# Two decoder layers on one core: V of two heads at once, a moved rope key, and another order of the sparse-attention items

## The chip, the cores and the metric

The kernel runs on one core of a Trainium2 chip. Times are device microseconds (us) of one launch. The names of the engines are those of the profile: PE is TensorE (PEld its weight load), DVE is VectorE, ACT is ScalarE, POOL is GpSimd, SP is the engine that issues most DMAs.

## What is computed

Two decoder layers over 512 tokens of width 1024, float32. Layer 0 mixes tokens with multi-head latent attention (MLA), layer 1 with sparse attention (an indexer picks 128 keys for each query). Each layer then attends to 256 memory tokens and runs a SwiGLU FFN; each sub-layer is followed by a scaled residual and a layer norm. Cut to the parts that the change touches:

```python
def mla_mixer(x, pos, w_in, q_norm, w_uq, kv_norm, w_ukv, w_o):
    h = x @ w_in
    c_q = h[..., :512]; c_kv = h[..., 512:768]; k_rope = h[..., 768:]
    q = rms_norm(c_q, q_norm) @ w_uq
    kv = rms_norm(c_kv, kv_norm) @ w_ukv
    ...

def dsa_mixer(x, pos, rel_bias, w_in, w_o):     # 16 heads, 4 KV heads
    ...
    _, sel = lax.top_k(score, 128)
    logits = einsum(q, k[sel]) * 64 ** -0.5 + rel_bias[bucket]
    o = softmax(logits) @ v[sel]
    return o @ w_o

def memory_cross_attention(x, mem, w_q, w_kv, w_o):   # 4 heads of 256
    q = (x @ w_q).reshape(b, s, 4, 256)
    kv = (mem @ w_kv).reshape(b, 256, 2, 4, 256)
    p = softmax(einsum(q, kv[:, :, 0]) * 256 ** -0.5)
    return einsum(p, kv[:, :, 1]).reshape(b, s, 1024) @ w_o
```

## The kernel before

Every large product is made of two fp32r parts: `split` (L98) lets ScalarE cast the high half (L99) and VectorE, or GpSimd where it is asked for, subtract the low half (L101), and `mm3` (L121) issues three matmuls, high by high (L122), high by low (L123) and low by high (L124). `chunk` (L108) loads a 128x1024 piece of a weight by a DMA on SP's queue into one of three `raw` buffers and splits it into `wh` and `wl` (five each). Working tiles come from the pools `t2` (39 of 128x512) and `t8` (9 of 128x2048); PSUM has four banks "a" and four banks "b". Each engine runs its instructions in the order in which the program was scheduled, and waits for its operands.

The front (from L169): x and the weight `w_ckv` come in slices, four steps `c` of two k-slices each; `ps2` are the four token tiles of c_kv and of the rope key (304 columns). `trig` (L449) makes sine and cosine on VectorE in steps. Then 8 copies on ScalarE (L521) and four transposes (L522) make the rope key `pkb`; four chunks of `w_cq` are loaded; for each token tile, 24 matmuls make `psq[tt]`, and `rms_t` (L527) normalises (L533) and transposes (L536) c_kv of this tile and c_q of the one before.

Cross-attention (`cross`, L733): for each head, `scores` with the softmax, the next head's Q projection (`q_proj`), the next head's K and V (`xa_kv`, L714), then `pv`, which first normalises and transposes P and then multiplies. K is two chunks of `xa_k`, V two chunks of `xa_v`; the V matmuls have 256 columns:

```python
        pv = bank("a", (P, 2, 256))
        for mt in range(2):
            for k in range(NK):
                mm3(pv[:, mt], ..., (w[0][:, k % 4], w[1][:, k % 4]), ...)
```

Sparse attention: 16 items of four heads each, item i is query tile i // 4 and KV head i % 4. `dsa_scores` (s) adds mask and bias and runs the softmax's first steps (L420 on VectorE, L426 on ScalarE), `dsa_t` (t) normalises, transposes (L1041) and splits P, `dsa_pv` (p) multiplies by V and sorts the heads (L1060 to L1077). The first items run inside the eight turns `j` that project Q: `steps` says which. In each turn five top-k steps of the masks (L978, L979) are put on VectorE, and `stack_q_pool` (L922) lets GpSimd subtract the low halves of two Q tiles (L927, L928):

```python
    steps = {2: "s0", 3: "t0", 4: "s1 p0", 5: "t1", 6: "s2 p1", 7: "t2"}
```

After the turns come s3, p2, s4, t3, and then the loop over the rest. `dsa_bias` (L1004) reads an item's bias from DRAM, for the first four items ahead of time into a `t2` tile, for the others at the scores into a `t8` tile.

## Time and profile before

| what | value |
|---|---|
| median of 3 runs | 1540.42 us (1538.08 to 1541.06) |
| the profiled execution | 1538.13 us |
| its span | 1536.3 us, 20733 instructions |
| PE busy | 1503.6 us (98%), 7902 matmul records |
| DVE busy | 994.9 us (65%) |
| ACT busy | 650.2 us (42%) |
| POOL busy | 303.9 us (20%) |
| DMA | 166.45 MB, mean 108 GB/s |

The page of a profile gives for each engine the time in which it was busy, and for groups of instructions their count, busy time and mean. A timeline row is one instruction or a run of equal ones: its start, its length, and in brackets how long the engine stood idle before and what released it. Matmuls are pipelined, so a matmul's own length is more than the step from one start to the next, and it is the steps that add up. PEclk is the clock that TensorE was granted, as a share of full speed.

### The profile page before, as it was taken

The numbers are of one execution on the slowest core, as the hardware profiler recorded it, in microseconds if no ns is written. First come the engines' busy times: TensorE is split into PE (matmuls) and PEld (weight loads), VectorE is DVE, ScalarE is ACT, GpSimd is POOL, SyncE is SP. The second block draws the span as 40 slices with busy tenths as digits, with TensorE's granted clock in tenths as the row PEclk, the third lists the DMA queues.
The fourth block names the chain that finished last, engine by engine and source line by source line (L and its number), as shares of the span: only waits on it lengthen the run. The fifth ranks groups of instructions, "written<-read, shape, count | busy, mean of one in ns | idle before, by whom it ended". The sixth has DMA issues, their size and how long they took to land.

```text
span 1536.3 us, 20733 instructions
## 1 busy us (share of the span) xinstructions
PE 1503.6 (98%) x7902; PEld 1283.5 (84%) x7902; DVE 994.9 (65%) x1741; ACT 650.2 (42%) x1158; POOL 303.9 (20%) x299
## 2 busy tenths in 40 slices
PE   8999999999999999999999989999999999999997
PEld 7788889988898888888888787898988888888886
DVE  7787868454746665654668988675448465656545
ACT  5677753343233333332246577344332433333230
POOL 1222001000032331400024653000002322324002
PEclk9999999999999999999999999999999999999999
DMA  6233424323333232233242147333323233222221
GB/s 214 71 98 107 155 83 134 125 85 97 124 97 101 77 124 97 96 97 108 84 138 87 51 158 240 110 119 102 110 94 125 83 110 98 102 94 90 97 96 55
DMA packets 51417, 166.45 MB, mean 108 GB/s; under 512 B 5300, under 2 KB 11972, under 8 KB 49268
## 3 DMA queue, kind: packets, MB, share of 16 engines
q1 hardware_dynamic: 50740, 164.18, 32.6%
q8 instruction: 62, 1.02, 0.3%
q10 hardware_dynamic: 576, 0.93, 0.2%
q14 instruction: 39, 0.32, 0.1%
HBM read 160.86 MB, written 9.47 MB: 111 GB/s over the span
## 4 chain that ended last, share of the span: by engine, by line
PE 88%; DVE 5%; ACT 3%; DMA 2%; issue 1%; POOL 1%; SPq 0%; POOLq 0%; DVEq 0%; ACTq 0%
PE ps L122 27%; PE ps L123 27%; PE ps L124 27%; DVE t L101 2%; PE ps L336 1%; ACT wh L99 1%; ACT t L426 1%; ACT t L99 1%; DMA raw<-in_w_cq_dram 1%; PE ps L1043 1%; PE ps L644 1%; DMA t<-in_xT_dram 1%; PE ps L1060 0%; POOL wl L101 0%; DMA t<-scr 0%
## 5 line engine op out<-in xcount | busy, mean ns | idle before, releaser
L122 PE MATMUL ps<-t,wh 128*128 128x512 f32 (+1 forms) x1256 | 456.2, 364 | 3.5 <-DVE t L101 3.4
L123 PE MATMUL ps<-t,wh 128*128 128x512 f32 (+1 forms) x1256 | 455.2, 362 | 0.8 <-DVE t L101 0.8
L124 PE MATMUL ps<-t,wl 128*128 128x512 f32 (+1 forms) x1256 | 454.9, 362 | 0.0
L99 ACT CAST wh<-raw 128x1024 fp32r<-128x1024 f32 (+3 forms) x219 | 227.4, 1038 | 450.0 <-PE ps L123 167.1
L101 DVE TENSOR_TENSOR wl<-raw,wh 128x1024 fp32r<-128x1024 f32 (+2 forms) x198 | 253.2, 1280 | 218.0 <-ACT wh L99 216.3
L122 PE MATMUL ps<-wh,t 128*128 128x512 f32 (+3 forms) x838 | 305.4, 364 | 1.1 <-ACT t L426 0.9
L123 PE MATMUL ps<-wl,t 128*128 128x512 f32 (+3 forms) x838 | 303.1, 362 | 1.2 <-DVE wl L101 1.2
L124 PE MATMUL ps<-wh,t 128*128 128x512 f32 (+3 forms) x838 | 303.0, 362 | 0.2 <-DVE t L101 0.2
L122 PEld LDWEIGHTS ps<-t,wh 128*128 128x128 f32 x1256 | 237.1, 189 | 41.5 <-DVE t L101 5.5
L123 PEld LDWEIGHTS ps<-t,wh 128*128 128x128 f32 x1256 | 237.2, 189 | 37.0 <-DVE t L101 1.3
L124 PEld LDWEIGHTS ps<-t,wl 128*128 128x128 f32 x1256 | 237.1, 189 | 36.6
L122 PEld LDWEIGHTS ps<-wh,t 128*128 128x128 f32 x838 | 158.5, 189 | 25.1 <-ACT t L426 1.3
L123 PEld LDWEIGHTS ps<-wl,t 128*128 128x128 f32 x838 | 158.4, 189 | 24.6 <-DVE wl L101 1.4
L124 PEld LDWEIGHTS ps<-wh,t 128*128 128x128 f32 x838 | 158.4, 189 | 24.0 <-DVE t L101 0.4
L99 ACT CAST t<-ps 128x512 fp32r<-128x512 f32 (+2 forms) x249 | 122.9, 525 | 129.3 <-PE ps L336 86.1
L279 POOL TENSOR_TENSOR sm<-sm,mhalf 128x1 f32<-128x1 f32 x32 | 28.6, 893 | 689.0 <-DVE sm L277 689.0
L101 DVE TENSOR_TENSOR t<-ps,t 128x512 fp32r<-128x512 f32 (+2 forms) x249 | 144.1, 607 | 20.3 <-ACT t L99 19.5
L99 ACT CAST wh<-t 128x1024 fp32r<-128x1024 f32 x56 | 58.9, 1052 | 141.9 <-PE ps L123 123.6
L101 DVE TENSOR_TENSOR wl<-t,wh 128x1024 fp32r<-128x1024 f32 x56 | 71.2, 1272 | 65.2 <-ACT wh L99 63.4
L863 DVE TENSOR_TENSOR t<-ps,t 128x512 f32<-128x512 f32 x44 | 30.4, 692 | 120.1 <-PE ps L124 120.1
L101 DVE TENSOR_TENSOR t<-t,t 128x512 fp32r<-128x512 f32 (+2 forms) x113 | 84.5, 751 | 23.0 <-ACT t L99 20.7
L99 ACT CAST t<-t 128x512 fp32r<-128x512 f32 (+2 forms) x113 | 64.5, 574 | 56.2 <-POOL t L797 33.6
(178 smaller groups left out, 1654.5 us busy)
## 6 DMA issues: line engine op xcount, KB each, us to landing
raw<-in_ffn_in_dram SPq DMA_DIRECT2D x88, 512.0 KB, 3.5
t<-in_ffn_dg_dram SPq DMA_DIRECT2D x16, 1024.0 KB, 5.0
raw<-in_xa_k_dram SPq DMA_DIRECT2D x16, 512.0 KB, 3.5
raw<-in_xa_v_dram SPq DMA_DIRECT2D x16, 512.0 KB, 3.9
raw<-in_xa_q_dram SPq DMA_DIRECT2D x16, 512.0 KB, 3.9
raw<-in_xa_o_dram SPq DMA_DIRECT2D x16, 512.0 KB, 3.4
raw<-in_ffn_dl_dram SPq DMA_DIRECT2D x12, 512.0 KB, 3.4
scr<-vscr SPq DMA_DIRECT2D x16, 319.5 KB, 4.4
```

What stands on the lines that cost most here:

```text
L99: nc.scalar.copy(h, src)
L101: (eng or nc.vector).tensor_tensor(l, src, h.bitcast(F32), op=ALU.subtract)
L122: nc.tensor.matmul(ps, st[0], mv[0], start=start, stop=False, skip_group_check=more)
L123: nc.tensor.matmul(ps, st[0], mv[1], start=False, stop=False, skip_group_check=more)
L124: nc.tensor.matmul(ps, st[1], mv[0], start=False, stop=stop, skip_group_check=more)
L279: nc.gpsimd.tensor_tensor(b, a, mhalf, op=ALU.pow)
L336: nc.tensor.transpose(pt[:, k], x_of(tt)[:, 512 * n + P * k:512 * n + P * k + P], ident)
L426: nc.scalar.activation(Sx, src, AF.Exp, bias=nb, scale=scale, accum_out=self.sm[:, i:i + 1])
L644: nc.tensor.transpose(pt[:, P * qt:P * qt + P], Ss[qt][:, P * kb:P * kb + P], ident)
L863: nc.vector.tensor_tensor(sg, pu, sg, op=ALU.mult)
L1043: nc.tensor.transpose(pt[:, P * i:P * i + P], Ss[i][:, P * kb:P * kb + P], ident)
```

## The change

Three parts. In the front, `w_ckv` is laid out with its eight k-slices side by side and loaded in four DMAs of 1, 2, 3 and 2 slices, all on ScalarE's queue, into the three `raw` buffers; the positions and constants are loaded right after x; and the rope key's copies and transposes become `rope_key()`, called after the first token tile's `psq` and `rms_t`. In cross-attention, `xa_kv` makes V for two heads at once (for an even head, four chunks of two k-slices by 512 columns), and `turned`, the normalise and transpose of P, runs before the next head's `xa_kv`, with only the products left in `pv`. In sparse attention, item 0 starts one turn later, item 4's bias is read at turn 4 into two `t2` tiles, and after the turns the order is s4, s3, s5, p2, t3, then the loop without its s5.

```diff
--- before.py
+++ after.py
@@ -167,20 +167,24 @@
...
-    def pairs_of(tile_):
-        return tile_[:, 0:2 * NC0].rearrange("p (k m) -> p k m", k=2)
-
-    raw_w = [pairs_of(wp.tile([P, 1024], F32, tag="raw", name=nm("raw"), bufs=3)) for _ in range(3)]
+    def threes(tag, dt, bufs=5):
+        ts = [wp.tile([P, 1024], dt, tag=tag, name=nm(tag), bufs=bufs) for _ in range(3)]
+        return [t[:, 0:3 * NC0].rearrange("p (k m) -> p k m", k=3) for t in ts]
+
+    raw_w = threes("raw", F32, 3)
     xr = A["xT"].rearrange("c p (k t) -> c p k t", k=2)
-    wr = A["w_ckv"].rearrange("c p (k m) -> c p k m", k=2)
-    for i in range(2):
+    wr = A["w_ckv"].rearrange("p (k m) -> p k m", k=NK)
+    for i, ks in enumerate((slice(0, 1), slice(1, 3))):
         nc.sync.dma_start(raw_x[0][:, i], xr[0, :, i])
-        nc.scalar.dma_start(raw_w[0][:, i], wr[0, :, i])
+        nc.scalar.dma_start(raw_w[0][:, ks], wr[:, ks])
     nc.sync.dma_start(raw_x[0][:, 2:4], xr[1])
-    nc.scalar.dma_start(raw_w[1], wr[1])
-    nc.scalar.dma_start(raw_w[2], wr[2])
+    nc.scalar.dma_start(raw_w[1], wr[:, 3:6])
     nc.sync.dma_start(raw_x[1][:, 0:2], xr[2])
+    nc.scalar.dma_start(raw_w[2][:, 0:2], wr[:, 6:8])
     nc.sync.dma_start(raw_x[1][:, 2:4], xr[3])
+    posi = t2(I32)
+    nc.sync.dma_start(posi, A["positions"].broadcast_to((P, S)))
+    nc.sync.dma_start(cst, A["consts"])
...
@@ -484,45 +488,44 @@
...
     ps2 = [bank("b") for _ in range(NT)]
+    whs, wls = threes("wh", FR), threes("wl", FR)
+    w_parts = {0: (0, 0, 1), 1: (0, 1, 3), 2: (1, 0, 3), 6: (2, 0, 2)}
     for c in range(4):
         h, l = XT[c // 2]
-        if c == 3:
-            raw_w.append(pairs_of(wp.tile([P, 1024], F32, tag="raw", name=nm("raw"), bufs=3)))
-            nc.sync.dma_start(raw_w[3], wr[3])
-        rx, rw = raw_x[c // 2], raw_w[c]
-        wh = pairs_of(wp.tile([P, 1024], FR, tag="wh", name=nm("wh")))
-        wl = pairs_of(wp.tile([P, 1024], FR, tag="wl", name=nm("wl")))
+        rx = raw_x[c // 2]
         step = 1 if c == 0 else 2
         for i in range(0, 2, step):
             k0 = 2 * (c % 2) + i
             split(h[:, k0:k0 + step], l[:, k0:k0 + step], rx[:, k0:k0 + step])
-            sw = slice(i, i + step)
-            split(wh[:, sw], wl[:, sw], rw[:, sw])
+            if 2 * c + i in w_parts:
+                t, a, b = w_parts[2 * c + i]
+                split(whs[t][:, a:b], wls[t][:, a:b], raw_w[t][:, a:b])
         for i in range(2):
             k = 2 * c + i
             xh, xl = k_of(XT, k)
             for tt in range(NT):
                 ts_ = ts_of(tt)
-                mm3(ps2[tt][:, 0:NC0], (xh[:, ts_], xl[:, ts_]), (wh[:, i], wl[:, i]), k == 0, k == NK - 1)
-    posi = t2(I32)
-    nc.sync.dma_start(posi, A["positions"].broadcast_to((P, S)))
-    nc.sync.dma_start(cst, A["consts"])
+                mm3(ps2[tt][:, 0:NC0], (xh[:, ts_], xl[:, ts_]), (whs[k // 3][:, k % 3], wls[k // 3][:, k % 3]),
+                    k == 0, k == NK - 1)
     steps = trig()
     for _ in range(2):
         next(steps)
...
-    pkb = bank("a")
-    for tt in range(NT):
-        kr = t2(F32, (P, 2, 2, 32))
-        for a in range(2):
-            c0 = 256 + 16 * a
-            nc.scalar.copy(kr[:, a], ps2[tt][:, c0:c0 + 32].unsqueeze(1).broadcast_to((P, 2, 32)))
-        nc.tensor.transpose(pkb[:, ts_of(tt)], kr.rearrange("p a b c -> p (a b c)"), ident)
     pk = t2()
-    nc.scalar.copy(pk, pkb)
     wcq = [chunk(A["w_cq"][c], (P, 2, 512)) for c in range(4)]
+
+    def rope_key():
+
+        pkb = bank("a")
+        for tt in range(NT):
+            kr = t2(F32, (P, 2, 2, 32))
+            for a in range(2):
+                c0 = 256 + 16 * a
+                nc.scalar.copy(kr[:, a], ps2[tt][:, c0:c0 + 32].unsqueeze(1).broadcast_to((P, 2, 32)))
+            nc.tensor.transpose(pkb[:, ts_of(tt)], kr.rearrange("p a b c -> p (a b c)"), ident)
+        nc.scalar.copy(pk, pkb)
...
@@ -569,6 +572,8 @@
         rms_t(ps2[tt], 256, tt, gkv[:, 0:256], ckv)
         if tt:
             rms_t(psq[tt - 1], 512, tt - 1, gq, cq)
+        if tt == 0:
+            rope_key()
         if tt < 2:
             next(steps)
@@ -719,15 +724,20 @@
...
-        ws = [chunk(A["xa_v"][i, hd, c], (P, 4, 256)) for c in range(2)]
-        pv = bank("a", (P, 2, 256))
-        for mt in range(2):
-            for k in range(NK):
+        if hd % 2:
+            return Kt, None
+        ws = [chunk(A["xa_v"][i, hd // 2, c], (P, 2, 512)) for c in range(4)]
+        pvs = [bank("a") for _ in range(2)]
+        for k in range(NK):
+            w = ws[k // 2]
+            for mt in range(2):
                 ms = slice(P * mt, P * mt + P)
-                w = ws[k // 4]
-                mm3(pv[:, mt], (m[k][0][:, ms], m[k][1][:, ms]), (w[0][:, k % 4], w[1][:, k % 4]), k == 0, k == NK - 1)
-        Vt = (t2(FR, (P, 2, 256)), t2(FR, (P, 2, 256)))
-        split(Vt[0], Vt[1], pv)
+                mm3(pvs[mt], (m[k][0][:, ms], m[k][1][:, ms]), (w[0][:, k % 2], w[1][:, k % 2]), k == 0, k == NK - 1)
+        Vt = []
+        for pv in pvs:
+            v = (t2(FR), t2(FR))
+            split(v[0], v[1], pv)
+            Vt.append(v)
         return Kt, Vt
@@ -756,9 +766,8 @@
...
-        def pv(hd, sx):
+        def turned(sx):
             Ss = sx.normalise()
-            Vt = kvs[hd][1]
             PT = []
...
+            return PT
+
+        def pv(hd, PT):
+            Vt = kvs[hd // 2 * 2][1]
             for dt in range(2):
                 po = bank("a")
-                ds_ = slice(P * dt, P * dt + P)
+                ds_ = slice(256 * (hd % 2) + P * dt, 256 * (hd % 2) + P * dt + P)
                 for mb in range(2):
-                    mm3(po, (Vt[0][:, mb, ds_], Vt[1][:, mb, ds_]), PT[mb], mb == 0, mb == 1)
+                    mm3(po, (Vt[mb][0][:, ds_], Vt[mb][1][:, ds_]), PT[mb], mb == 0, mb == 1)
...
@@ -781,8 +794,10 @@
             Ss = scores(hd, Q)
             if hd < 3:
                 Q = q_proj(hd + 1)
+            PT = turned(Ss)
+            if hd < 3:
                 kvs[hd + 1] = xa_kv(i, hd + 1, m)
-            pv(hd, Ss)
+            pv(hd, PT)
@@ -1004,11 +1019,17 @@
     def dsa_bias(qt, g):
         n = P * (qt + 1)
         c0 = 127 + 384 - 128 * qt
-        bt = t8(F32, (P, 4, 512)) if qt else t2(F32, (P, 4, P))
-        read = nc.sync.dma_start(bt[:, :, 0:n],
-                                 scr[bass.ds(r * (1 + qt), 1), 4 * g:4 * g + 4, :, c0:c0 + n].rearrange("a h p k -> p (a h) k"))
+        if (qt, g) == (1, 0):
+            bts = [t2(F32, (P, 2, 256)) for _ in range(2)]
+        else:
+            bts = [t8(F32, (P, 4, 512)) if qt else t2(F32, (P, 4, P))]
+        m = 4 // len(bts)
+        for i, bt in enumerate(bts):
+            read = nc.sync.dma_start(bt[:, :, 0:n],
+                                     scr[bass.ds(r * (1 + qt), 1), 4 * g + m * i:4 * g + m * i + m, :,
+                                         c0:c0 + n].rearrange("a h p k -> p (a h) k"))
         reads.append(read)
-        return bt
+        return [bts[i // m][:, i % m, 0:n] for i in range(4)]
@@ -1018,15 +1039,15 @@
         n = P * (qt + 1)
         N = max(n, 256)
         ts_ = slice(P * qt, P * qt + P)
-        bt = dsa_bias(qt, g) if qt else first_bias[g]
-        sx = Softmax([bt[:, i, 0:n] for i in range(4)])
+        bt = dsa_bias(qt, g) if 4 * qt + g > 4 else first_bias[4 * qt + g]
+        sx = Softmax(bt)
         for i in range(4):
             ps = bank("b")
...
-            sx.exp(i, ps[:, :n], 0.125, bt[:, i, 0:n])
+            sx.exp(i, ps[:, :n], 0.125, bt[i])
@@ -1091,7 +1112,7 @@
...
-    steps = {2: "s0", 3: "t0", 4: "s1 p0", 5: "t1", 6: "s2 p1", 7: "t2"}
+    steps = {3: "s0", 4: "t0 s1", 5: "p0 t1", 6: "s2 p1", 7: "t2"}
...
-        if j < 4:
-            first_bias.append(dsa_bias(0, j))
+        if j < 5:
+            first_bias.append(dsa_bias(j // 4, j % 4))
...
+    run_s(4)
     run_s(3)
+    run_s(5)
     run("p2")
-    run_s(4)
     run_t(3)
     for i in range(3, 16):
         a = 1 if i < LA else 0
         if i != LA:
-            run_s(i + 1 + a)
+            if i > 3:
+                run_s(i + 1 + a)
             run_t(i + a)
@@ -1170,7 +1193,8 @@
     w = I["mla_w_in"][0]
     f["w_cq"] = _tm(w[:, :512], 2, 512)[0]
-    f["w_ckv"] = _tm(np.concatenate([w[:, 512:800], w[:, 768:784]], 1), 2, NC0)[0]
+    ckr = np.concatenate([w[:, 512:800], w[:, 768:784]], 1)
+    f["w_ckv"] = ckr.reshape(NK, P, NC0).transpose(1, 0, 2).reshape(P, NK * NC0)
@@ -1194,7 +1218,7 @@
-    f["xa_v"] = np.stack([_tm(I["xa_w_kv"][i][:, 1024:], 4, 256) for i in range(2)])
+    f["xa_v"] = np.stack([_tm(I["xa_w_kv"][i][:, 1024:], 2, 512) for i in range(2)])
```

Line numbers of the changed kernel are some 3 to 21 higher from the rope key on (L420 is L424 there, L533 is L536, L1027 is L1048, L1041 is L1062, L1060 is L1081).

TensorE at the end of the c_kv products (`ps_130`, `ps_133`); before, the rope key's transposes (L522) stand between them and the first Q products (128x512):

```order
L124 MATMUL ps_130<-wh_227,t_10_118 128x304
L522 MATMUL ps_279<-ident,t_37_280 128x128
L522 MATMUL ps_279<-ident,t_38_284 128x128
L522 MATMUL ps_279<-ident,t_39_288 128x128
L122 MATMUL ps_322<-wh_300,t_7_115 128x512
L522 MATMUL ps_279<-ident,t_40_292 128x128
L123 MATMUL ps_322<-wl_301,t_7_115 128x512
```

and with the change:

```order
L124 MATMUL ps_133<-wh_136,t_11_121 128x304
L122 MATMUL ps_298<-wh_276,t_8_118 128x512
L123 MATMUL ps_298<-wl_277,t_8_118 128x512
L124 MATMUL ps_298<-wh_276,t_9_119 128x512
L122 MATMUL ps_298<-wh_276,t_8_118 128x512
L123 MATMUL ps_298<-wl_277,t_8_118 128x512
```

The four transposes have left this place; they now follow the first tile's 24 products and its two c_kv transposes.

VectorE at the same time; before, up to the low half of the fourth chunk of w_cq (`wl_319`; `wl_307` and `wl_313` are the second and third, lines 466 to 472 are steps of `trig`):

```order
L472 SCALAR_TENSOR_TENSOR t_32_261<-t_33_262,t_32_261 128x512
L101 TENSOR_TENSOR wl_307<-raw_304,wh_306 128x1024
L472 SCALAR_TENSOR_TENSOR t_32_261<-t_33_262,t_32_261 128x512 x2
L466 TENSOR_SCALAR t_33_262<-t_32_261 128x512
L101 TENSOR_TENSOR wl_313<-raw_310,wh_312 128x1024
L470 TENSOR_SCALAR t_33_262<-t_33_262 128x512
L472 SCALAR_TENSOR_TENSOR t_32_261<-t_33_262,t_32_261 128x512 x3
L101 TENSOR_TENSOR wl_319<-raw_316,wh_318 128x1024
```

and with the change (`wl_295` is the fourth chunk, `wl_283` and `wl_289` the second and third, the steps of `trig` have lines 470 to 476):

```order
L476 SCALAR_TENSOR_TENSOR t_29_255<-t_30_256,t_29_255 128x512
L101 TENSOR_TENSOR wl_289<-raw_286,wh_288 128x1024
L476 SCALAR_TENSOR_TENSOR t_29_255<-t_30_256,t_29_255 128x512 x2
L470 TENSOR_SCALAR t_30_256<-t_29_255 128x512
L474 TENSOR_SCALAR t_30_256<-t_30_256 128x512
L476 SCALAR_TENSOR_TENSOR t_29_255<-t_30_256,t_29_255 128x512 x2
L101 TENSOR_TENSOR wl_295<-raw_292,wh_294 128x1024
```

One of the last three steps of L472 (L476 now) has moved behind the fourth chunk; the other steps still stand ahead of it.

TensorE where the eight turns of sparse attention end; before, item 2's transposes (L1041), then item 3's scores (128x256, two matmuls for a head: L1027, L1028), with item 2's products (L1060) behind them:

```order
L1041 MATMUL ps_11567<-ident,t_1578_11099 128x128 x4
L1027 MATMUL ps_11579<-t_1554_10981,t_1667_11459 128x256
L1028 MATMUL ps_11579<-t_1554_10981,t_1667_11459 128x256
L1027 MATMUL ps_11584<-t_1554_10981,t_1668_11460 128x256
L1028 MATMUL ps_11584<-t_1554_10981,t_1668_11460 128x256
L1027 MATMUL ps_11589<-t_1554_10981,t_1693_11555 128x256
L1028 MATMUL ps_11589<-t_1554_10981,t_1693_11555 128x256
L105 MATMUL ps_11567<-t_1699_11572,identn 128x512
L1027 MATMUL ps_11594<-t_1554_10981,t_1694_11556 128x256
L1028 MATMUL ps_11594<-t_1554_10981,t_1694_11556 128x256
L1060 MATMUL ps_11603<-t_1699_11572,t_1454_10444 128x512
```

and with the change, where item 4's scores (three matmuls for a head: L1047 is the mask) come first:

```order
L1062 MATMUL ps_11469<-ident,t_1575_10997 128x128 x4
L1047 MATMUL ps_11481<-t_1537_10795,identr 128x256
L1048 MATMUL ps_11481<-t_1544_10833,t_1552_10888 128x256
L1049 MATMUL ps_11481<-t_1544_10833,t_1552_10888 128x256
L1047 MATMUL ps_11487<-t_1537_10795,identr 128x256
L1048 MATMUL ps_11487<-t_1544_10833,t_1552_10888 128x256
L1049 MATMUL ps_11487<-t_1544_10833,t_1552_10888 128x256
L1047 MATMUL ps_11493<-t_1537_10795,identr 128x256
L1048 MATMUL ps_11493<-t_1544_10833,t_1552_10888 128x256
L1049 MATMUL ps_11493<-t_1544_10833,t_1552_10888 128x256
L1047 MATMUL ps_11499<-t_1537_10795,identr 128x256
L1048 MATMUL ps_11499<-t_1544_10833,t_1552_10888 128x256
```

Item 3's scores follow behind these twelve matmuls.

## Rows read from the trace of the kernel before

**Rows 1.** The page: engines' busy time; two groups (count | busy us, mean ns)

```profile
PE 1503.6 (98%) x7902; PEld 1283.5 (84%) x7902; DVE 994.9 (65%) x1741; ACT 650.2 (42%) x1158; POOL 303.9 (20%) x299
...
L99 ACT CAST wh<-raw 128x1024 fp32r<-128x1024 f32 (+3 forms) x219 | 227.4, 1038 | 450.0 <-PE ps L123 167.1
...
L101 DVE TENSOR_TENSOR wl<-raw,wh 128x1024 fp32r<-128x1024 f32 (+2 forms) x198 | 253.2, 1280 | 218.0 <-ACT wh L99 216.3
```

**Rows 2.** Waits of TensorE: total us, times, longest us

```profile
PE ps L522 <- ACT t L521: 3.6, 1, 3.6
...
PE ps L1027 <- POOL t L927: 3.2, 2, 2.8
...
PE ps L123 <- DVE wl L101: 1.2, 1, 1.2
```

**Rows 3.** TensorE's timeline, front: start us, us, line, tiles [idle before <- releaser]

```profile
25.10 0.79 PE L522 MATMUL ps<-ident,t 128*128 128x128 f32 x3 [3.63 <-ACT t L521]
...
25.64 0.48 PE L122 MATMUL ps<-wh,t 128*128 128x512 f32 x1
...
29.46 0.42 PE L122 MATMUL ps<-wh,t 128*128 128x512 f32 x1
...
39.46 0.48 PE L122 MATMUL ps<-wh,t 128*128 128x512 f32 x1
```

**Rows 4.** Timelines of TensorE (one row) and GpSimd (two), sparse attention

```profile
889.53 0.49 PE L1027 MATMUL ps<-t,t 128*128 128x256 f32 x1 [2.77 <-POOL t L927]
...
888.22 1.26 POOL L927 TENSOR_TENSOR t<-t,t 64x512 fp32r<-64x512 f32 x1
...
889.55 1.27 POOL L928 TENSOR_TENSOR t<-t,t 64x512 fp32r<-64x512 f32 x1
```

**Rows 5.** Windows, front: us, busy us by engine, PEclk, DMA share, GB/s

```profile
2.00:12.00 10.00, 8.47 (x45) 7.46 (x46) 5.12 (x9) 6.79 (x10) 1.05 (x4) 1.00 0.97 356
12.00:38.00 26.00, 22.32 (x120) 19.31 (x119) 22.52 (x39) 13.01 (x29) 2.52 (x4) 0.93 0.54 178
26.00:30.00 4.00, 4.00 (x13) 3.13 (x12) 3.86 (x7) 1.90 (x6) 0.00 (x0) 0.57 0.44 166
40.00:50.00 10.00, 10.00 (x48) 8.31 (x47) 5.58 (x12) 4.59 (x11) 1.64 (x3) 1.00 0.01 2
```

**Rows 6.** Windows, sparse attention, and one row of VectorE's timeline there

```profile
824.60:890.00 65.40, 60.73 (x290) 50.12 (x289) 62.72 (x184) 39.97 (x82) 39.19 (x35) 1.00 0.27 84
...
890.00:894.00 4.00, 3.79 (x19) 3.05 (x18) 2.07 (x10) 2.12 (x9) 0.82 (x1) 0.62 0.00 0
...
891.71 0.29 DVE L420 CUSTOM_DVE_ANT_0 t<-ps,t 128x128 f32<-128x128 f32 x1 [1.13 <-PE ps L1028]
```

**Rows 7.** TensorE's timeline: 256 columns in cross-attention, 512 in the FFN

```profile
289.74 0.28 PE L122 MATMUL ps<-t,wh 128*128 128x256 f32 x1
...
301.13 0.28 PE L124 MATMUL ps<-wh,t 128*128 128x256 f32 x1
...
480.13 0.39 PE L122 MATMUL ps<-t,wh 128*128 128x512 f32 x1
...
490.11 0.39 PE L124 MATMUL ps<-t,wl 128*128 128x512 f32 x1
```

**Rows 8.** VectorE's timeline, softmax of one head of cross-attention

```profile
279.35 0.76 DVE L424 TENSOR_REDUCE sm<-ps 128x1 f32<-128x256 f32 x2 [0.51 <-PE ps L124]
...
282.38 1.14 DVE L438 TENSOR_SCALAR t<-t,sm 128x256 f32<-128x256 f32 x4
```

**Rows 9.** DMA issues of the page; landing times of the chunks of dsa_o

```profile
raw<-in_xa_v_dram SPq DMA_DIRECT2D x16, 512.0 KB, 3.9
...
DMA to landing us min/median/max: 3.6/5.5/8.3
```

**Rows 10.** VectorE's timeline, front

```profile
22.62 1.23 DVE L101 TENSOR_TENSOR wl<-raw,wh 128x1024 fp32r<-128x1024 f32 x1 [0.81 <-ACT wh L99]
...
26.28 1.22 DVE L101 TENSOR_TENSOR wl<-raw,wh 128x1024 fp32r<-128x1024 f32 x1
```

## The prediction

> **What bounds the kernel now.** I read the page first, then the list of what TensorE waits for, then the two places where it waits longest, then the engine it waits for there. TensorE is busy 1503.6 of 1536.3 us [rows 1], so there are two sources of time: less work for TensorE, or one of its few waits. The list of waits shows what the second can give: 3.6 us once behind a ScalarE copy of line 521 (front), 3.2 us in two pieces behind GpSimd's line 927 (sparse attention), 1.2 us behind a VectorE subtraction (front) [rows 2]. None of them lies in cross-attention. After the two longest TensorE goes on at about half its pace: in the front nine matmuls of 512 columns take 25.64 to 29.46, 0.42 us each [rows 3], and in sparse attention it restarts at 889.53 after a wait of 2.77 [rows 4]; the granted clock behind them is 0.57 and 0.62 [rows 5, 6], so a part of these stretches ran at 1.2 instead of 2.4 GHz.
>
> **Cross-attention: V for two heads at once.** Each layer has 4 heads x 2 memory tiles x 8 k-slices x 3 = 192 matmuls of 256 columns for V, 384 in both; the change makes 192 of 512 columns of them. One head's K and V stand at 289.74 to 301.13: 96 starts, 95 steps of 0.1199 us. The 512-column pace is at 480.13 to 490.11: 45 starts, 44 steps of 0.2268 us [rows 7]. So 384 x 0.1199 = 46.0 us become 192 x 0.2268 = 43.5: **-2.5 us**. At 2.4 GHz, 256 columns last 0.1067 us and 512 last 0.2133; both rows are some 0.0133 us above that, so what is saved is a fixed part of each matmul, and half of these matmuls go. The Trainium skill ("TensorE: Matmul & The Clock Gate", section "Back-to-back issue gap") gives the isolated warm gap as the columns over 2.4 GHz plus 2.5 ns; by it V would give 192 x 2.5 ns = 0.5 us and the sum below would be -4.5. The rows of this kernel, 119.9 and 226.8 ns where that formula says 109 and 216, do not agree with it, and I take the rows.
>
> Turning P (normalise, 8 transposes) now comes before the next head's K and V, behind the next Q projection: 2 x 8 x 3 = 48 matmuls x 0.2268 = 10.9 us. That is the cover for the softmax, which VectorE has from 279.35 to 283.5, 4.2 us [rows 8]; so I cost it at nothing. Without cover it would be those 4.2 us for three heads of each layer. The last head had no cover before and has none now. The loads change their order, not their number: K,K,V,V,V,V for an even head, K,K for an odd one. A 512 KB chunk feeds TensorE for 12 x 0.2268 = 2.72 us (V) or 24 x 0.1199 = 2.88 (K). Three buffers that each need 3.9 us to land [rows 9] and 1.04 + 1.28 us to split [rows 1] deliver one per (3.9 + 2.32)/3 = 2.07 us. Nothing; the bound is a rival.
>
> **Front.** Today the 8 copies of the rope key (line 521) are queued on ScalarE behind the cast of the fourth w_cq chunk, which waits for its load. TensorE's transposes of that key stand ahead of the Q projection, so it is idle 3.63 us until 25.10, and then nine matmuls take 3.82 us instead of 9 x 0.2268 = 2.04 [rows 3]. Together 5.4 us. Nothing needs the rope key so early, and the change puts the Q projection of the first tile there. What is late next is VectorE: it is busy 22.52 of 26 us from 12 to 38 [rows 5], with sine steps and low halves of weights in turn. The order shows that the low half of the fourth chunk still has those steps ahead of it, all but one of some 0.7 us (three of them stand between the splits at 22.62 and 26.28 [rows 10], with one shorter step, in the 2.5 us that these leave). Today it starts at 26.28 [rows 10] and ends 1.1 later, at 27.4. Without that step, and with the gap of 0.81 (a cast that came late) [rows 10] closed because the chunks get their buffers sooner, it ends at about 25.8.
>
> TensorE meanwhile: the c_kv sums end at 25.10 - 3.63 = 21.5 [rows 3] and some 0.85 us sooner if most of the wait of 1.2 for the low half of w_ckv [rows 2] goes with the smaller first slices, so at 20.6. 18 matmuls on three chunks take 4.1 us, to 24.7. A wait of 1.1 us for VectorE; the last six end at 27.2. Then the two c_kv transposes wait for VectorE's line 536 with a GpSimd step in between (my estimate: 0.85 us), the four rope transposes take 0.4, and the second tile's 24 matmuls 5.4: 33.9. There the first tile's own transposes wait for VectorE's line 536 once more. By the order seven sine steps, a split and the norms stand ahead of it, some 7 us behind 27.8, and with their gaps they end near 36.2; third tile from 37.0. Today that starts at 39.46 [rows 3]: **-2.5 us**. From 40 on VectorE has air (5.58 of 10 us [rows 5]), so the gain stays. Bounds: if a wait takes the place of nearly all that is removed, -1; if VectorE keeps up and nothing waits, 5.4 + 0.85 = 6.2.
>
> The DMAs: four of w_ckv instead of five, the positions (256 KB) and constants ahead of w_cq on SP's queue. The 16 DMA engines are busy 0.97 of 2 to 12 us [rows 5] and the bytes are the same, so this gives nothing beyond the 0.85 us above.
>
> **Sparse attention.** Today item 3's scores (line 1027) wait 2.77 us until 889.53 for GpSimd, which stacks the last Q heads (line 927, from 888.22) behind the casts of item 1 [rows 4]. The change puts item 4, whose Q and bias are there, in front. But VectorE, with the top-k steps, is busy 62.72 of 65.40 us from 824.6 to 890 [rows 6], without a gap of any size in its last stretch, and its order is fixed: it takes item 4's first softmax step only behind the last turn's top-k steps, a little before 890. TensorE would fill its four banks with item 4 by 888 and stand idle 2 us there. What can come back is VectorE's own idle time behind that: 4.00 - 2.07 = 1.9 us from 890 to 894, 1.13 of it in one wait for line 1028 [rows 6]. Some of it returns as waits for banks and for line 928, which ends at 890.8 [rows 4] as before. I take **-1.5 us**, nearer to 1.9 than to nothing, since items 4, 3 and 5 then lie ready together. Item 0's later start removes TensorE waits of about 1 us, but VectorE has no gap there: nothing. The two bias tiles read for item 4 at turn 4 move the same bytes and leave one large buffer free; the later reads shift along. Bounds: 0 and -2.
>
> **Sum.** -2.5 - 2.5 - 1.5 = -6.5 us. The profiled execution took 1538.1 us (span 1536.3 and 1.8 around it), 2.3 under the median of the three runs, 1540.4. That gives 1531.6 for a run like it, and off the median **1533.9 us**.
>
> **Rivals.**
> *VectorE keeps what TensorE gets.* In front and sparse attention each wait comes back at the next low half or mask step, and only V pays: 1540.4 - 2.5 = 1537.9. For it: VectorE's share [rows 5, 6]. Against: its own gap of 1.9 us, and that the half pace behind 25 us is TensorE's loss alone. Chance 0.2.
> *All waits go.* Front 6.2, V 2.5, sparse 1.9: 10.6 us, 1529.8. For it: the waits are single, and what released them is moved. Against: VectorE's share. Chance 0.13.
> *Bursts of six loads.* K,K,V,V,V,V outrun the three buffers. A load plus 2.32 us, over 3, must stay under 2.72: it decides from a load of 5.9 us on. xa_v lands in 3.9, but the chunks of dsa_o, the same size, take 3.6 to 8.3 [rows 9]. At 8.3, 3.54 - 2.72 = 0.82 us for the four late chunks of four bursts, 13 us: 1547, slower than before. It outweighs the gain of 6.5 from 0.41 us a chunk on, a load of 7.1. Against: xa_v's median. Chance 0.06.
> *Columns alone count.* If a wide V matmul costs 2 x 0.1199, V gives nothing: 1536.4. The formula of the page named above comes near to this. The 512-column rows speak against it; 0.03.
>
> **How the numbers follow.** My forecast has 0.58. About 0.2% (3.1 us) is what a measurement of this kernel can tell from no change: faster is under 1537.3, slower over 1543.5. Faster: the forecast, all waits gone, columns alone and a tenth of the first rival, 0.58 + 0.13 + 0.03 + 0.02 = 0.76. Same: the rest of the first rival, 0.18. Slower: the bursts, 0.06. The range goes from 1528.5 (just beyond all waits gone) to 1539 (just beyond V alone); it leaves out the bursts and the tails.
>
> **What would show it.** Right: 192 V matmuls at steps of 0.227 us; a TensorE wait near 25 us that is under 2 us; the third Q tile at 37; at 888 a wait of some 2 us, with the stretch behind it 1 to 2 us earlier than front and V account for. Wrong: TensorE waits for wh or wl in cross-attention (bursts); a granted clock under 0.8 at 24 to 30 us (the front's stall moved, not removed); VectorE's gaps behind 890 as large as now.

## The result, and the profile after

The changed kernel takes 1530.58 us (median of 6 runs, 1529.54 to 1531.58), the kernel before 1538.93 beside it (median of 6, 1537.51 to 1541.06): a ratio of 0.9945, 95% interval 0.9932 to 0.9958, 8.4 us faster. Forecast were 1533.9 us and a gain of 6.5. The profiled execution has a span of 1528.7 us, 7.6 less than the 1536.3 shown of before.

The page of the changed kernel, its line of busy times, answers to [rows 1]:

```profile
PE 1500.5 (98%) x7710; PEld 1273.7 (83%) x7710; DVE 994.7 (65%) x1740; ACT 651.4 (43%) x1157; POOL 303.5 (20%) x299
```

TensorE is busy 3.1 us less. What it waits for (columns as in [rows 2]):

```profile
PE ps L105 <- ACT t L104: 3.7, 3, 3.3
...
PE ps L340 <- DVE t L336: 1.5, 2, 0.8
...
PE ps L539 <- DVE t L536: 0.9, 1, 0.9
```

Line 927 has left the list, and the copies of the rope key (line 521, now 526) are down from 3.6 us to 0.5. A wait for a ScalarE cast in sparse attention (L104, 3.3 us in one piece) has come in.

TensorE's timeline in the front, for [rows 3] (start us, us, tiles, idle before):

```profile
7.67 0.46 PE L124 MATMUL ps<-wh,t 128*128 128x304 f32 x1
...
9.19 0.46 PE L124 MATMUL ps<-wh,t 128*128 128x304 f32 x1
...
11.82 0.30 PE L124 MATMUL ps<-wh,t 128*128 128x304 f32 x1
...
12.65 0.30 PE L124 MATMUL ps<-wh,t 128*128 128x304 f32 x1
...
28.11 0.44 PE L539 MATMUL ps<-ident,t 128*128 128x128 f32 x2 [0.51 <-ACT t L526]
...
35.74 0.66 PE L539 MATMUL ps<-ident,t 128*128 128x128 f32 x4 [0.91 <-DVE t L536]
36.15 0.47 PE L122 MATMUL ps<-wh,t 128*128 128x512 f32 x1
```

The third Q tile starts at 36.15 instead of 39.46. From 7.67 to 9.19 lie six steps of 304 columns, 0.253 us each; from 11.82 to 12.65 six of 0.138. In this execution the first 20 of the c_kv matmuls ran at the slower pace, which is 304 columns at 1.2 GHz (0.253).

Windows of the changed kernel, for [rows 5] (TensorE, its weight load, VectorE, ScalarE, GpSimd, PEclk, DMA share, GB/s), and of the stretch behind the new wait:

```profile
2.00:12.00 10.00, 9.72 (x41) 9.09 (x42) 5.38 (x9) 6.53 (x9) 1.05 (x5) 1.00 0.99 372
12.00:38.00 26.00, 24.59 (x141) 21.56 (x141) 22.59 (x40) 15.55 (x35) 2.46 (x5) 1.00 0.50 172
26.00:30.00 4.00, 3.49 (x19) 2.56 (x18) 3.52 (x8) 2.12 (x12) 0.71 (x1) 1.00 0.34 131
40.00:50.00 10.00, 10.00 (x58) 8.62 (x57) 6.87 (x13) 6.56 (x13) 1.65 (x3) 1.00 0.25 66
870.00:874.00 4.00, 0.87 (x4) 0.38 (x2) 3.92 (x14) 1.49 (x5) 0.98 (x3) 1.00 0.00 0
874.00:878.00 4.00, 3.85 (x13) 3.21 (x14) 3.02 (x10) 1.75 (x4) 3.14 (x3) 0.61 0.00 0
```

The granted clock at 26 to 30 us is 1.00 instead of 0.57; VectorE still has 22.59 of the 26 us from 12 to 38. At 2 to 12 us the column shows 1.00 beside matmuls at half pace: that early, the pace is the better witness. Behind the new wait from 870 on the clock falls to 0.61. TensorE where that wait ends:

```profile
874.14 0.50 PE L105 MATMUL ps<-t,identn 128*128 128x512 f32 x1 [3.27 <-ACT t L104]
```

The starts of one and the same TensorE instruction, in each program less its start in the profile of before, show where the time went (worked out from the timelines of the profiled executions; "E" are the runs below; "third Q tile" is read at a transpose just ahead of it):

| us against before at | third Q tile | end of the layer norm behind cross-attention 0 | FFN 0, its middle | start of sparse attention | its item 8 | its end | end of cross-attention 1 |
|---|---|---|---|---|---|---|---|
| (time in before) | 39.2 | 404.5 | 525.8 | 823.9 | 905.8 | 968.7 | 1129.7 |
| changed kernel | -3.3 | -5.7 | -4.8 | -4.8 | -3.6 | -5.9 | -7.7 |
| the same again (E11) | -2.9 | -5.1 | -5.2 | -5.2 | -3.9 | -6.3 | -8.6 |
| before again (E8) | -1.1 | -1.0 | -0.2 | -0.3 | -0.2 | +0.5 | +0.5 |
| front only (E1) | -2.9 | -3.0 | -3.0 | -3.0 | -1.7 | -2.4 | -2.7 |
| cross-attention only (E2) | -1.0 | -3.4 | -2.5 | -2.5 | -1.2 | -3.4 | -6.0 |
| V only (E5) | -0.4 | +0.8 | +1.6 | +1.5 | +1.5 | -0.8 | +1.1 |
| sparse part only (E3) | -0.7 | -0.7 | +0.2 | +0.2 | +1.5 | +1.4 | +1.1 |
| bias tiles only (E4) | -0.6 | -0.6 | +0.2 | +0.1 | +0.2 | -1.6 | -1.8 |
| bias tiles again (E12) | -0.4 | -0.1 | +0.2 | +0.1 | +0.3 | -1.1 | -1.4 |
| 12 warm-up matmuls (E6) | -3.4 | -5.8 | -4.9 | -5.0 | -5.1 | -7.0 | -8.8 |
| old turns (E7) | -3.3 | -5.8 | -4.9 | -5.0 | -5.7 | -8.0 | -9.8 |
| old turns again (E10) | -3.1 | -5.2 | -4.3 | -4.4 | -5.1 | -7.1 | -9.8 |
| old turns, p2 first (E9) | -3.0 | -5.2 | -4.3 | -4.4 | -3.3 | -5.6 | -7.4 |

So the changed kernel gains 3.3 us in front, 2.4 in the first cross-attention, loses 0.9 in the FFN, loses 1.3 in the first half of sparse attention, wins 2.4 in its second half and 1.8 by the end of the second cross-attention. All of this is counted from one profile of before, which is the latest of its kind in the front: the seven profiles that have the front of before lie there at 0 to -1.1, mean -0.6, and the seven with the new front at -2.9 to -3.4, mean -3.1. So the new front is worth about 2.5 us rather than 3.3.

### The profile page after: what moved, and what is told of

The parts are those of the page before. It is cut to its first block, busy times and chain, and to the rows that moved or that the text cites. A ratio compares the mean times of both kernels' runs of the same rounds, so it can differ in the third digit from the quotient of the medians.

```text
span 1528.7 us, 20371 instructions
## 1 busy us (share of the span) xinstructions
PE 1500.5 (98%) x7710; PEld 1273.7 (83%) x7710; DVE 994.7 (65%) x1740; ACT 651.4 (43%) x1157; POOL 303.5 (20%) x299
## 3 DMA queue, kind: packets, MB, share of 16 engines
q10 hardware_dynamic: 576, 1.25, 0.2%
## 4 chain that ended last, share of the span: by engine, by line
PE 85%; DVE 10%; ACT 2%; DMA 2%; issue 1%; POOL 0%; SPq 0%; POOLq 0%; DVEq 0%; ACTq 0%
PE ps L122 26%; PE ps L123 26%; PE ps L124 26%; DVE t L101 2%; DVE t L994 1%; DVE m L993 1%; PE ps L340 1%; DVE wl L101 1%; PE ps L1064 1%; ACT t L430 1%; ACT wh L99 1%; PE ps L649 1%; DMA t<-in_xT_dram 1%; PE ps L1081 0%; PE ps L775 0%
## 5 line engine op out<-in xcount | busy, mean ns | idle before, releaser
L99 ACT CAST wh<-raw 128x1024 fp32r<-128x1024 f32 (+2 forms) x218 | 227.2, 1042 | 443.9 <-PE ps L123 164.3
L122 PE MATMUL ps<-wh,t 128*128 128x512 f32 (+3 forms) x774 | 294.4, 380 | 0.2
L123 PE MATMUL ps<-wl,t 128*128 128x512 f32 (+3 forms) x774 | 292.2, 377 | 0.1
L124 PE MATMUL ps<-wh,t 128*128 128x512 f32 (+3 forms) x774 | 291.8, 377 | 0.0
L122 PEld LDWEIGHTS ps<-wh,t 128*128 128x128 f32 x774 | 146.5, 189 | 26.0 <-ACT wh L99 0.4
L124 PEld LDWEIGHTS ps<-wh,t 128*128 128x128 f32 x774 | 146.3, 189 | 26.0
L123 PEld LDWEIGHTS ps<-wl,t 128*128 128x128 f32 x774 | 146.5, 189 | 25.5 <-DVE wl L101 0.5
L101 DVE TENSOR_TENSOR t<-t,t 128x512 fp32r<-128x512 f32 (+2 forms) x113 | 84.4, 750 | 28.0 <-ACT t L99 25.8
```

The costliest lines, as they stand in the source:

```text
L99: nc.scalar.copy(h, src)
L101: (eng or nc.vector).tensor_tensor(l, src, h.bitcast(F32), op=ALU.subtract)
L122: nc.tensor.matmul(ps, st[0], mv[0], start=start, stop=False, skip_group_check=more)
L123: nc.tensor.matmul(ps, st[0], mv[1], start=False, stop=False, skip_group_check=more)
L124: nc.tensor.matmul(ps, st[1], mv[0], start=False, stop=stop, skip_group_check=more)
```

## The experiments

**E1 to E4: each part alone.** The front's hunks, those of cross-attention, those of sparse attention, and of the last only the two bias tiles with the order of before (against E3; the loop runs s5 again):

```diff
-    steps = {3: "s0", 4: "t0 s1", 5: "p0 t1", 6: "s2 p1", 7: "t2"}
+    steps = {2: "s0", 3: "t0", 4: "s1 p0", 5: "t1", 6: "s2 p1", 7: "t2"}
...
-    run_s(4)
     run_s(3)
-    run_s(5)
     run("p2")
+    run_s(4)
     run_t(3)
```

> The kernel before with the front's part alone. Theory A (the parts are independent): the third Q tile starts at about 36.2 us as with the whole change, 3.3 us earlier than 39.46, the rest of the program shifts by that and the time falls by about 3.3 us. Rival (the shift is eaten further on, where VectorE or a load sets the pace in latent attention): the third tile starts as early, but the end moves by less than 2 us.

> The kernel before with the cross-attention part alone. Theory A: 192 V matmuls at 0.227 us, and the cross-attention of each layer ends about 2.4 us earlier (1.25 from V, the rest from waits behind the softmax that the earlier turning of P removes); if the wait of 0.8 us at the first transposes of the FFN comes with it, -3.3 us in all, without it -4.8. Rival (columns alone count): V gives nothing, and the time falls by 2 us or less. Rival (bursts of six loads): TensorE waits for wh or wl in cross-attention.

> The kernel before with the sparse-attention part alone. Theory A: the stage up to about 900 us loses some 1.3 us (a new TensorE wait of about 3.3 us behind ScalarE's line 104 at 874, half the clock after it, VectorE idle 2.2 us at 897), the stage behind it gains some 2.4 us where waits for bias loads vanish; together -1.1 us. Rival (both come from the upstream shift of the other parts and not from this part): no new wait at 874, the bias waits near 932 and 941 stay, and the time moves by -1.5 us or 0.

> The kernel before with item 4's bias read at turn 4 into two t2 tiles, the order of all items as before. Theory A (the late gain is the large buffer that item 4 no longer takes): the waits near 932 and 941 vanish here too, the wait of 2.77 at 889.5 stays, and the time falls by about 2.4 us, more than with the whole sparse part. Rival (the late gain comes from the new order of items): the waits near 932 and 941 stay and the time is unchanged within 0.5 us.

| run | median us | ratio to before, 95% interval |
|---|---|---|
| E1 front | 1534.35 | 0.9978 (0.9968 to 0.9988) |
| E2 cross-attention | 1531.83 | 0.9961 (0.9947 to 0.9976) |
| E3 sparse attention | 1537.93 | 1.0005 (0.9995 to 1.0015) |
| E4 bias tiles | 1536.23 | 0.9996 (0.9986 to 1.0006) |

The median of before beside them was 1537.49. Front and cross-attention pay 3.1 and 5.7 us (by the intervals 1.8 to 4.9 and 3.7 to 8.1), the sparse part nothing that can be measured (+0.4); together -8.4, the whole gain. Each profile had its own surprise.

E1: the shift of 3.0 us is whole until sparse attention starts, and there 1.3 us are lost although not an instruction of this stage differs from before. Windows of E1 behind its wait for line 927 (886.54 here), and of before behind the same wait:

```profile
886.50:890.50 4.00, 3.36 (x13) 2.75 (x14) 2.06 (x7) 2.08 (x9) 1.27 (x1) 0.58 0.00 0
890.50:897.00 6.50, 6.50 (x44) 6.45 (x43) 5.24 (x24) 4.57 (x14) 3.44 (x6) 0.73 0.00 1
```

```profile
889.50:893.50 4.00, 3.76 (x15) 3.02 (x16) 2.07 (x7) 2.12 (x10) 1.27 (x1) 0.57 0.00 0
893.50:900.00 6.50, 6.50 (x55) 6.30 (x54) 6.39 (x27) 5.64 (x18) 3.51 (x6) 1.00 0.00 1
```

The granted clock is down to 0.58 and 0.57 for 4 us in both, and then in E1 at 0.73 for 6.5 us more, in before at 1.00. The wait is the same to 0.02 us; what its clock costs is not. E2, whose sparse attention is also that of before, loses the same 1.3 us (from -2.5 to -1.2), with 0.58 and 0.74 in these stretches.

E2 expected 3.3 or 4.8 and has 5.7. Cross-attention 0 gives the 2.4 (from -1.0 to -3.4), no wait for wh or wl appears, and V's matmuls go at the expected pace. The late wait of sparse attention (VectorE for a bias load near 932, shown below) is also gone, without any of the bias edit; so is it in E4, without the cross-attention part. In E3, with bias tiles and new order, it is there. E3 also has the new wait of 3.3 us for line 104 and loses 1.3 us up to item 8, as its theory A said, so that wait comes with the sparse part; the late gain that the same theory expected did not come. The row of VectorE, in before and in E3:

```profile
932.87 0.69 DVE L420 CUSTOM_DVE_ANT_0 t<-ps,t 128x512 f32<-128x512 f32 x1 [1.59 <-DMA t<-scr]
```

```profile
934.46 0.69 DVE L420 CUSTOM_DVE_ANT_0 t<-ps,t 128x512 f32<-128x512 f32 x1 [1.70 <-DMA t<-scr]
```

Both of my theories on it fall: that the buffer that item 4 leaves free is what removes it, and that the order does.

**E5: V of two heads, P turned after K and V as before.**

```diff
             if hd < 3:
                 Q = q_proj(hd + 1)
-            PT = turned(Ss)
-            if hd < 3:
                 kvs[hd + 1] = xa_kv(i, hd + 1, m)
-            pv(hd, PT)
+            pv(hd, turned(Ss))
```

> The kernel before with V of two heads at once, but P turned after K and V as before. Theory A (V pays 1.25 us a layer, the earlier turning the rest of the 2.4): cross-attention of layer 0 ends 1.25 us earlier than before, counted from its start, and the four waits of 0.2 to 0.6 us behind the softmax are still there. Rival (all of the 2.4 us comes from V): 2.4 us earlier, waits gone or not.

1538.82 us, ratio 1.0005 (0.9996 to 1.0015): nothing. Neither came: cross-attention 0 is 1.2 us longer than in before (from -0.4 to +0.8). TensorE in E5, behind the transposes of P of an even head:

```profile
300.28 1.04 PE L770 MATMUL ps<-ident,t 128*128 128x128 f32 x8
301.98 1.00 PE L122 MATMUL ps<-t,t 128*128 128x256 f32 x5 [0.67 <-ACT t L99]
303.45 0.47 PE L122 MATMUL ps<-t,t 128*128 128x512 f32 x1 [0.47 <-DVE t L101]
```

and in the changed kernel at the same head, where the products of P and V follow K's last matmul and no wait stands anywhere near:

```profile
297.74 0.28 PE L122 MATMUL ps<-t,wh 128*128 128x256 f32 x1
...
298.10 0.40 PE L122 MATMUL ps<-t,t 128*128 128x512 f32 x1
```

An odd head now has only K to compute. With P turned late, 0.8 us of transposes are all that lies between K's last matmul and the scores that need K's split, and K's and P's splits queue up together (three casts on ScalarE from 301.35 on, three subtractions on VectorE from 302.62 on). So TensorE waits 0.67 us for ScalarE at the scores and 0.47 for VectorE behind them (0.83 and 0.65 more from start to start than the pace), twice a layer. These and two smaller ones cost 0.83 + 0.65 + 0.21 + 0.84 + 0.66 + 0.31 = 3.5 us in layer 0; the gaps of before cost 0.21 + 0.22 + 0.21 + 0.59 = 1.2. Without them, V itself gives 1.2 - (3.5 - 1.2) = -1.1 us in this layer, near the 1.25 of the matmul rows. With the turn ahead no gap of over 0.15 us is left: the products of the previous head stand between K and its use. The second cross-attention of E5 is 1.9 us longer than in before (from -0.8 to +1.1). That the time is unchanged nevertheless is due to the late wait, which E5 has lost too (-2.3 in the second half of sparse attention), though its sparse part is that of before.

**E6: 12 instead of 8 warm-up matmuls** (`WARM = 12`) in the changed kernel.

> The changed kernel with 12 instead of 8 warm-up matmuls on TensorE, so that it is busy until about 6.9 us. In the changed kernel the first 22 of the c_kv matmuls take 0.254 us instead of 0.139. Theory A (VectorE sets the front's end): these matmuls run at 0.139, the c_kv sums end some 2 us earlier, and the third Q tile still starts within 0.6 us of 36.2, as TensorE waits longer for VectorE's low halves near 25 us and for line 536. Rival (TensorE's clock sets it): the third Q tile starts 2 us earlier and the time falls by 2 us.

1531.43 us, ratio 0.9959 (0.9944 to 0.9973), against 0.9945 of the changed kernel: no gain. TensorE in E6:

```profile
6.54 0.31 PE L123 MATMUL ps<-wl,t 128*128 128x304 f32 x1
...
7.38 0.30 PE L123 MATMUL ps<-wl,t 128*128 128x304 f32 x1
...
26.82 0.50 PE L123 MATMUL ps<-wl,t 128*128 128x512 f32 x1 [1.94 <-DVE wl L101]
...
36.03 0.48 PE L122 MATMUL ps<-wh,t 128*128 128x512 f32 x1
```

The c_kv matmuls run at 0.14 us from the second on (6.54 to 7.38, seven starts) and end sooner, and TensorE then waits 1.94 us for VectorE's low half of the fourth chunk; the third Q tile starts at 36.03, 0.1 us from the changed kernel. Theory A holds: VectorE sets the end of the front. That the 12 matmuls brought the full pace is not shown: E1, E9, E10 and E11 have it with eight.

This run shows one more thing. It has the wait at 870 of the changed kernel, but the clock behind it stays:

```profile
870.00:874.00 4.00, 0.74 (x4) 0.28 (x2) 3.92 (x14) 1.58 (x5) 1.09 (x4) 1.00 0.00 0
874.00:878.00 4.00, 3.98 (x20) 3.37 (x21) 3.86 (x12) 2.60 (x6) 3.92 (x4) 1.00 0.00 0
```

1.00 where the changed kernel had 0.61, and its first half of sparse attention costs -0.1 us instead of +1.3. What the changed kernel loses against before is the clock behind the wait. VectorE is busy 3.92 of 4.00 us during the wait itself.

**E7, E10: the table of turns of before, with s4, s3, s5 kept.**

```diff
-    steps = {3: "s0", 4: "t0 s1", 5: "p0 t1", 6: "s2 p1", 7: "t2"}
+    steps = {2: "s0", 3: "t0", 4: "s1 p0", 5: "t1", 6: "s2 p1", 7: "t2"}
```

> The changed kernel with the table of turns of before (item 0 from turn 2 on), with s4, s3, s5 after the turns kept. Theory A (the later start of items 0 and 1 crowds items 1 and 2 in the turns and makes the wait of 3.27 us at 874): that wait is gone, the stage to 900 us gains 1 to 3 us against the changed kernel and 0.5 to 1.9 against before. Rival (the tail s4, s3, s5 causes the loss): the wait at 874 is gone or not, and the stage to 905 is as late as in the changed kernel, within 0.5 us.

> The changed kernel with the table of turns of before, once more, beside the changed kernel on one chip. Theory A: 2.1 us shorter than the changed kernel, as its stage to 905 us was; the late waits near 932 are as absent as in the changed kernel. Rival (the difference was one execution's): within 0.7 us.

1528.86 us, ratio 0.9943 (0.9926 to 0.9959), and again 1528.68, 0.9944 (0.9930 to 0.9957). Its first half of sparse attention is 0.7 us shorter than that of before, twice. The wait of 3.3 us is gone, and so is every fall of the clock behind 870; windows of E7:

```profile
870.00:880.00 10.00, 10.00 (x50) 8.40 (x49) 9.68 (x29) 4.32 (x13) 7.02 (x5) 1.00 0.11 32
880.00:890.00 10.00, 8.81 (x65) 7.80 (x64) 9.68 (x40) 7.85 (x28) 4.33 (x7) 1.00 0.38 127
```

So the two edits of the order work against each other: the tail s4, s3, s5 pays 0.7 us, where 1.5 was forecast, and the new table of turns costs 2.0 in the two profiles of the changed kernel (and about 0.6 where the clock held, in E6). The 0.7 is counted from before. Against E1 and E2, which keep the order of before and lose 1.3 us behind its wait, it would be 2.0; how much of the tail's worth is clock is open.

**E9: with p2 ahead of s5** in that tail.

```diff
     run_s(4)
     run_s(3)
-    run_s(5)
     run("p2")
+    run_s(5)
     run_t(3)
```

> The changed kernel with the table of turns of before and the tail s4, s3, p2, s5, t3 (p2 ahead of s5). Theory A (VectorE's idle 1.9 us at 895 waits for GpSimd's casts of p2, which come late because p2's sorting stands behind s5's softmax steps on VectorE): the sorting comes some 1.4 us earlier, the idle time shrinks to about 0.5 us, and the stage to 905 us ends 1 to 1.4 us earlier than with the old turns alone. Rival (the order of the tail does not matter, another wait takes its place): the stage ends within 0.4 us of that.

1529.51 us, ratio 0.9948 (0.9935 to 0.9962). Theory A falls, and so does the rival: item 8 starts 1.8 us later than in E10 (-3.3 against -5.1). The medians differ by 0.8 us, and their intervals overlap. GpSimd's casts do come sooner, but so does the weight split behind them. VectorE in E9, and GpSimd in the same stretch:

```profile
893.47 2.55 DVE L998 TENSOR_SCALAR t<-t 128x512 fp32r<-128x512 f32 x1
895.95 0.68 DVE L101 TENSOR_TENSOR t<-ps,t 128x512 fp32r<-128x512 f32 x1
```

```profile
893.39 2.35 POOL L101 TENSOR_TENSOR wl<-raw,wh 128x1024 fp32r<-128x1024 f32 x1
```

and the same instruction of VectorE in E10, where that split starts at 895.87, well behind it:

```profile
893.08 0.43 DVE L998 TENSOR_SCALAR t<-t 128x512 fp32r<-128x512 f32 x1
```

The mask instruction of line 998 takes 2.55 us under the split instead of 0.43 and ends 0.28 us after it. So VectorE's split of P, for which TensorE waits, starts at 895.95 as against 895.75: nothing is won there, and TensorE has by now done the transposes that fill part of this stretch in E10 (eight from 893.20). TensorE in E9:

```profile
896.68 3.15 PE L1062 MATMUL ps<-ident,t 128*128 128x128 f32 x16 [2.26 <-DVE t L101]
```

```profile
894.00:898.00 4.00, 1.74 (x12) 1.46 (x11) 3.97 (x5) 1.21 (x3) 2.28 (x2) 0.93 0.02 4
898.00:902.00 4.00, 4.00 (x21) 3.65 (x21) 2.01 (x11) 2.67 (x9) 3.26 (x6) 0.65 0.15 31
```

One wait of 2.26 us, with the clock at 0.65 behind it; E10 has three there, of 1.08, 0.44 and 0.24, and 1.00 throughout. The wait has changed its owner.

**E8, E11, E12: before, the change and the bias tiles once more.**

> The kernel before once more, nothing changed. Theory A (the bias load issued near 926 us lands after 5.1 to 6.9 us as it comes, and the wait of 1.6 us at 932 with it; the wait of 0.8 us in the FFN at 424 likewise): one or both differ from the first profile, with the program the same. Rival (they belong to the program): both are as in the first profile, 1.6 us and none.

> The changed kernel once more, nothing else. Theory A (the late wait near 932 comes with a load that lands after more than 6 us, in some executions and not in others): no prediction for this execution. Rival (it belongs to the program): no wait near 932, the load lands after about 5.2 us as in the first profile; the stage to 905 us again loses 1.3 us, with the wait of 3.3 us at 874.

> The kernel before with item 4's bias in two t2 tiles, once more. Theory A (the late wait comes and goes with the execution): it may be there now (1.1 to 1.8 us near 932, the load landing after 6.3 us or more). Rival (it belongs to the program, and this edit removes it): the load again lands after about 5.1 us, without a wait.

E8 (one run, 1538.61 us) has the late wait as before, 1.79 us, and in the FFN a wait of 0.7 us that the first profile did not have. E11 (1530.24 us, ratio 0.9956, 0.9942 to 0.9970) has no late wait, as in the first profile, and no wait in the FFN, where the first one had it. E12 (1536.58 us, ratio 0.9992, 0.9982 to 1.0001) has no late wait, as E4. So the 0.9 us in the FFN come and go with the execution; theory A is right there. The late wait belongs to the program, as far as two profiles of each of four programs can tell (twice there in before, twice absent in the change, with the bias tiles and with the old turns); there the rival is right. What decides it is not settled: the wait goes when a bias load that is issued near 926 us lands in about 5.2 us instead of 6.4 to 7, with the same loads issued around it.

The loss in the first half of sparse attention is in E11 as in the first profile, 1.3 us, with the wait of 3.25 us at 873.8 and a clock of 0.64 behind it. Its front is not as in the first profile. TensorE in E11:

```profile
6.54 0.30 PE L124 MATMUL ps<-wh,t 128*128 128x304 f32 x1
...
6.96 0.30 PE L124 MATMUL ps<-wh,t 128*128 128x304 f32 x1
...
26.12 0.50 PE L123 MATMUL ps<-wl,t 128*128 128x512 f32 x1 [1.43 <-DVE wl L101]
...
36.57 0.47 PE L122 MATMUL ps<-wh,t 128*128 128x512 f32 x1
```

With the same program and eight warm-up matmuls the c_kv matmuls run at 0.14 us from 6.54 on, their sums end at 20.3 instead of 22.1, and TensorE then waits 1.43 us for VectorE; the third Q tile starts 0.4 us later than in the first profile. That says the same as E6, without any edit.

E10 and E11 ran side by side: 1528.25 to 1529.76 against 1529.60 to 1532.10. **The changed kernel with the old table of turns is the fastest of all, about 1.5 us ahead of the change**, though the intervals of their ratios overlap.

## Why the prediction was right, point by point

- **The front, -2.5 forecast; -3.3 and -2.9 in two profiles, -2.9 alone, 2.5 between the means of the two fronts.** The mechanism held: the low half of the fourth chunk ends at 25.6 (25.8 forecast), the rope key and the fall of the clock are off the path, VectorE sets the third Q tile. The step "the c_kv sums end [...] some 0.85 us sooner" held in E1, E9, E10 and E11 (20.3 to 20.5, 1.0 to 1.1 us sooner), and there the wait of 1.1 us that should follow at 24.7 is 1.2 to 1.4 us. In the first profile of the change it did not: 20 matmuls ran at 1.2 GHz, the sums end at 22.1, some 0.65 us later than before, and no wait shows at 24.7. The half pace is not the new slices' doing: E2 and E4, with the front of before, have it for 16 matmuls and more. What brings it is open. One loss stands in the place of the other; the sum hardly feels it. VectorE's row of the changed kernel:

```profile
24.43 1.22 DVE L101 TENSOR_TENSOR wl<-raw,wh 128x1024 fp32r<-128x1024 f32 x1
```

- **V, -2.5 forecast.** The pace is right. TensorE in the changed kernel, a V block of two heads: from 323.52 to 330.32 lie 30 steps of 0.2267 us.

```profile
323.52 0.39 PE L122 MATMUL ps<-wh,t 128*128 128x512 f32 x1
323.75 0.39 PE L123 MATMUL ps<-wl,t 128*128 128x512 f32 x1
...
330.32 0.39 PE L122 MATMUL ps<-wh,t 128*128 128x512 f32 x1
```

  And E5 less its waits gives 1.1 a layer. The rule for isolated matmuls of the Trainium skill that was weighed there ("TensorE: Matmul & The Clock Gate", section "Back-to-back issue gap"), 0.5 us in all, is not borne out in this stream: a fixed part of 13 ns a matmul goes, not one of 2.5. The same section's cold gap, columns over 1.2 GHz, does agree: 0.253 us for 304 columns.
- **Turning P earlier, forecast at nothing: the step of cross-attention that failed.** I checked that it had cover, and not what it uncovers. It gives a little more than 1.1 us in the first layer against before, and without it the two cross-attentions are 1.2 and 1.9 us longer than in before, in spite of V for two heads (E5). The reason is in the order: K's split needs something between K and the scores.
- **Sparse attention, -1.5 forecast, 0 in the clock (E3).** Three terms were wrong, and cancelled in part. The tail pays 0.7, not 1.5 (E7, E10). The forecast took it from VectorE's idle 1.9 us behind 890. The wait of some 2 us at 888 that was to show it did not come, and the idle time was not won: VectorE idles 2.19 us in one piece there in the changed kernel and 1.92 in E10, as much as before, which the forecast had named as a sign of being wrong. VectorE in the changed kernel:

```profile
897.28 1.29 DVE L101 TENSOR_TENSOR t<-ps,t 128x512 fp32r<-128x512 f32 x2 [2.19 <-PE ps L1082]
```

  "Item 0's later start [...]: nothing" was wrong: it costs 0.6 to 2. ScalarE's cast of item 1's P (L104) is queued behind item 2's second exp, which waits for VectorE, where item 0's sorting and top-k steps stand in between:

```profile
872.99 0.40 ACT L430 ACTIVATE t<-t,sm 128x128 f32<-128x128 f32 x1 [2.12 <-DVE sm L424]
...
873.51 0.59 ACT L104 CAST t<-ps 128x512 fp32r<-128x512 f32 x1
```

```profile
870.05 0.28 DVE L424 CUSTOM_DVE_ANT_0 t<-ps,t 128x128 f32<-128x128 f32 x1
...
872.66 0.28 DVE L424 CUSTOM_DVE_ANT_0 t<-ps,t 128x128 f32<-128x128 f32 x1
```

  The two softmax steps of item 2 lie 2.6 us apart on VectorE, and TensorE waits until the cast that stands behind them. And "the later reads shift along" was wrong: VectorE's late waits for bias loads, 1.6 us at 932.9 and 0.8 at 939.7 in before, are not in the changed kernel.
- **The sum.** -3.3 - 2.4 + 0.9 + 1.3 - 2.4 - 1.8 = -7.7, against 7.6 in the span; the medians give -8.4. That the forecast's -6.5 is so near is in part luck. Against this profile the front gave 0.8 more than forecast and the two cross-attentions 1.7 more, from turning P. In sparse attention two errors of opposite sign stand against each other: its first half was forecast at -1.5 and lost 1.3, 2.8 us off, and the second half, forecast at nothing, gave 2.4. The 0.9 us in the FFN come and go.
- **The rivals.** "VectorE keeps what TensorE gets" describes the first half of sparse attention well (E6: a new wait of 3.3 us, and the half ends as in before). All waits go: refuted, since a wait of 3.3 us came in. Bursts of six loads: no wait for wh or wl appears in cross-attention. Columns alone: refuted by the pace.

## What to carry to other kernels

A product that is computed for two consumers at once leaves one of them with less work ahead of its use: look what now covers the split or cast of that operand, and move finished work there in the same change, or the gain is eaten (E5). When a wait of TensorE is removed, ask which engine was busy through it: if that engine has no gap, the wait can move to another place (E9), and its cost then changes mainly with the clock behind it. Take a second profile of the same kernel before explaining 1 us: between two profiles of before the front moves by 1.1 us, and the FFN by 0.9 between two of the change. The first half of sparse attention moves by 1.3 between programs that do not differ there (E1 and E2 against before).
